# Two-layer encoder on one core: the last convolution block's taps as packed products on TensorE, and its input products moved between the first attention turns and the first scores

## The chip, the core and the metric

The program runs on one core of a Trainium2 chip. A core has five engines with a queue of instructions each, which it works off strictly in order: PE (TensorE, matrix products, whose results land in banks of an accumulator memory, PSUM, of 128 partitions by 512 float32), DVE (VectorE), ACT (ScalarE), POOL (GpSimd) and SP (SyncE, which here only starts DMA transfers). An instruction waits on semaphores for others; whatever is queued behind a waiting instruction on its engine waits too. The metric is the device time of one execution in microseconds (us).

## The reference, cut to what matters

Two layers on a sequence of 512 tokens with 1024 features. Each layer adds a gated feed-forward block (half weight), a "mix" of attention and convolution, and a second feed-forward block (half weight), and ends in a norm. The change is inside the mix:

```
h = rms_norm(x);  p = h @ w_in          # columns split: q latent, kv latent, k_pe, convolution
attn = mla_group(...)                    # 8 heads of 96, chunk-causal
u = a * sigmoid(g)                       # a, g: 512 channels each, from p
y[t, ch] = conv_b[ch] + sum_k conv_w[k, ch] * u[t - 30 + k, ch]     # 31 taps, causal, per channel
conv = silu(layer_norm(y))
x = x + concat(attn, conv) @ w_out
```

The convolution is depthwise: channel ch of y takes channel ch of u alone, at 31 shifts in time.

## The kernel before

Activations lie with features on the partitions and the 512 tokens along the free axis, so a shift in time is a shift along the free axis. The 512 convolution channels are four blocks of 128, named c0 to c3. A large product of float32 accuracy is made of three products with operands split into a high and a low part (`mm3`, L144, L145, L146); a projection of one block of 128 columns is 8 x 3 = 24 such products of 512 columns (`group`), and a weight tile takes a load on SP (L131), a cast on ACT (L133) and a subtraction on DVE or POOL (L139). For the first four tiles of w_out that subtraction is a second ACT pass (L136) and an accumulating DMA that POOL starts (L137).

The mix first runs its projections in the order of the string `SEQ`: q0 to q2, qo, k, kt, tt, uq, uk for attention (uk is `keys`, whose last step per token block is a power on POOL, `sck<-ssk`, L162, then the scaling of `kn` on DVE), and c0 to c3 for the convolution: `conv_in(c)` is two projections (48 products) and then `glu` (L510 DVE, L512 ACT, L514 and L516 DVE), which leaves u[c]. c0's products are the ones that come ahead of "R". Then come the heads, in a software pipeline over `step` (`ORDER` "t0s1p3v4o5"): in one step the code issues the turn of head step (L695, L700: transposes of q and kn on PE, evicted by ACT at L697 and DVE at L702), the scores of head step - 1 (L718, L719 on PE, row maximum L720 on DVE, exponential L724 on ACT), turn_p of head step - 3 (L739, L742), values of step - 4 (L752, L759) and turn_out of step - 5 (L770).

After the heads' code the convolution's taps are issued, as the string `CONV` = "DAAD" says for c0 to c3:

- Kind D: ACT writes weight times u plus bias into a PSUM bank of the tag "cv", which has one buffer (L787), DVE adds the 30 other taps into the bank one at a time (L791), and ACT copies it back (L801).
- Kind A: ACT writes the product of one tap into a buffer `pr` (L795; three buffers), and POOL adds it into y (L799). In c1 the adds from shift 16 on, and in c2 all of them, are told to issue only after the last `sck` of the keys.

Then POOL adds the four blocks (`ysum`, L813 to L815), a product with a matrix of ones takes the mean (`pm`, L817), and layer norm, silu and the products of w_out follow. `early` groups of w_out's attention half are put between these.

The order of each engine's queue is set when the program is built: a scheduler with a timeline of its own places the instructions by when it takes their operands to be ready. So code that stands after the heads, such as the taps, is spread between the heads' instructions. In the names below cv is a block's PSUM bank, r a general slot, pr and y as above, ps a PSUM bank, mx and sums the softmax's rows.

Of the kernel before, what the change touches and what calls it, by code (L numbers as in the profile page):

```python
# [7 lines left out]
FP = mybir.dt.float32  # L8
# [3 lines left out]
AF = mybir.ActivationFunctionType  # L12
# [3 lines left out]
P = 128  # L16
D = 1024
S = 512
L = 2
# [10 lines left out]
CK = 31  # L30
# [3 lines left out]
WC = 1024  # L34
# [3 lines left out]
FRB = 9  # L38
RING = 40
WIDE = 4  # L40
CONV = "DAAD"
PAUSE = 16
SEQ = "q0 R c1 q1 q2 qo k kt tt uq uk c2 c3"
POOLW = "wo"
QFOLD = 0
GLUP = 0
# [22 lines left out]

@with_exitstack  # L70
def encoder_kernel(ctx: ExitStack, tc: tile.TileContext, xT, consts, vecs, rgain, wgu1, wd1,
                   wcv, wql, wkl, wuq, wkv, wout, wgu2, wd2, out):
    nc = tc.nc
    PSUM = bass.MemoryType.PSUM
    cpool = ctx.enter_context(tc.tile_pool(name="const", bufs=1))
# [2 lines left out]
    wpool = ctx.enter_context(tc.tile_pool(name="w", bufs=4))  # L78
    rpool = ctx.enter_context(tc.tile_pool(name="rp", bufs=2))
    small = ctx.enter_context(tc.tile_pool(name="small", bufs=2))  # L80
    psum = ctx.enter_context(tc.tile_pool(name="psum", bufs=7, space=PSUM))
    uid = [0]

    def nm(s):
        uid[0] += 1
        return f"{s}{uid[0]}"

    def slot(dt=FP, w=S):
        return ring.tile([P, w], dt, tag="r", name=nm("r"))
# [4 lines left out]
    def bank():  # L94
        return psum.tile([P, S], FP, tag="ps", name=nm("ps"))
# [4 lines left out]
    V, A, G, T = nc.vector, nc.scalar, nc.gpsimd, nc.tensor  # L100
# [23 lines left out]
    def vv(l, name):  # L124
        o, w = VOFF[name]
        return vec[:, l, o:o + w]

    def load_w(src, w, kind="", two=False):
        raw = wpool.tile([P, WC], FP, tag="raw", name=nm("raw"), bufs=3)
        to = raw[:, :w]  # L130
        nc.sync.dma_start(out=to.rearrange("p (m c) -> p m c", m=2) if two else to, in_=src)  # L131
        hi = wpool.tile([P, WC], FR, tag="wh", name=nm("wh"))
        A.copy(hi[:, :w], raw[:, :w])  # L133
        lo = wpool.tile([P, WC], FR, tag="wl", name=nm("wl"))
        if kind == "sum":
            A.activation(lo[:, :w], raw[:, :w], AF.Copy, scale=-1.0)  # L136
            G.dma_start(out=lo[:, :w], in_=src, accum_op=ALU.add)  # L137
            return hi, lo
        (G if kind in POOLW.split() else V).tensor_tensor(lo[:, :w], raw[:, :w], hi[:, :w].bitcast(FP),  # L139
                                                          ALU.subtract)  # L140
        return hi, lo
# [6 lines left out]
    def split(src, w=S):  # L148
        hi, lo = slot(FR, w), slot(FR, w)
        A.copy(hi, src)  # L150
        V.tensor_tensor(lo, src, hi.bitcast(FP), ALU.subtract)
        return hi, lo
# [56 lines left out]
    def group(o, w, rhs, ks, n):  # L209

        for k in ks:
            c = slice(k * P, (k + 1) * P)
            mm3(o, w[0][:, c], w[1][:, c], rhs[k][0], rhs[k][1], k == 0, k == n - 1)
# [286 lines left out]
    def mix(l, gx, norm, done):  # L500
        with tc.tile_pool(name="k", bufs=4) as kpool:
            mix_body(kpool, l, gx, norm, done)

    def mix_body(kpool, l, gx, norm, done):
        u, order = [], {}
        ys = [None if kind == "D" else kpool.tile([P, S], FP, tag="y", name=nm("y"), bufs=2) for kind in CONV]

        def glu(pa, pg):
            tg = tmp()
            V.tensor_tensor(tg, pg, R, ALU.mult)  # L510
            sg = tmp()
            A.activation(sg, tg, AF.Sigmoid)  # L512
            ta = tmp()
            V.tensor_tensor(ta, pa, R, ALU.mult)  # L514
            uc = slot()
            (G if GLUP else V).tensor_tensor(uc, ta, sg, ALU.mult)  # L516
            u.append(uc)

        def conv_in(c):
            pp = []  # L520
            for j in range(2):
                ps = bank()
                group(ps, load_w(wcv[l, 2 * c + j], WC, f"c{c}"), gx, range(KD), KD)
                pp.append(ps)
            glu(*pp)
# [148 lines left out]
        rm = norm()  # L674
        for step in SEQ.split():
            if step == "R":
                R = norm()
# [85 lines left out]
        def turn_out(h):  # L763
# [6 lines left out]
                T.transpose(ps[:, t * P:(t + 1) * P], o[:, t * P:(t + 1) * P], ident)  # L770
            at.append(split(ps))

        STAGES = [({"t": turn, "s": scores, "p": turn_p, "v": values, "o": turn_out}[c], int(d)) for c, d in zip(ORDER[::2], ORDER[1::2])]
        for step in range(H + 6):
            for stage, lag in STAGES:
                if 0 <= step - lag < H:
                    stage(step - lag)


        with tc.issue_after(order["keys"]):  # L780
            wo = [load_w(wout[l, m], WC, "sum") for m in range(WOP)]
        cw, cb = vv(l, "cw"), vv(l, "cb")
        for c in range(4):
            kind = CONV[c]
            acc = psum.tile([P, S], FP, tag="cv", name=nm("cv"), bufs=1) if kind == "D" else ys[c]
            tap = lambda k: cw[:, c * CK + k:c * CK + k + 1]
            A.activation(acc, u[c], AF.Identity, scale=tap(CK - 1), bias=cb[:, c:c + 1])  # L787
            for k in range(CK - 2, -1, -1):
                s = CK - 1 - k
                if kind == "D":  # L790
                    V.scalar_tensor_tensor(acc[:, s:], u[c][:, :S - s], tap(k), acc[:, s:], ALU.mult, ALU.add)  # L791
                    continue
                pr = kpool.tile([P, S], FP, tag="pr", name=nm("pr"), bufs=3)
                if kind == "A":
                    A.activation(pr[:, s:], u[c][:, :S - s], AF.Copy, scale=tap(k))  # L795
                else:
                    G.tensor_scalar(pr[:, s:], u[c][:, :S - s], tap(k), None, ALU.mult)
                with tc.issue_after(order["keys"]) if s >= PAUSE or c > 1 else nullcontext():
                    order["conv"] = G.tensor_tensor(acc[:, s:], acc[:, s:], pr[:, s:], ALU.add).ins  # L799
            if kind == "D":  # L800
                A.copy(u[c], acc)  # L801
                ys[c] = u[c]
# [27 lines left out]
        cv = []  # L830
# [217 lines left out]
```

## Time and profile before

| what | value |
|---|---|
| runs, median (lowest to highest) | 1835.69 us (1835.47 to 1835.96), three runs |
| the profiled execution's own time | 1836.73 us |
| its span, first to last instruction | 1834.9 us |
| mean granted TensorE clock | 0.993 |
| busy: PE / DVE / ACT / POOL | 98% / 73% / 52% / 15% of the span |
| mix of layer 0: keys' last product issued | 431.73 us |
| mix of layer 0: turn of head 0 on PE | 453.72 us |
| mix of layer 0: first scores of head 3 on PE | 475.04 us |
| mix of layer 0: product `pm`, L817 | 518.22 us |

Times inside the run are counted from the span's start. A timeline row gives start, duration, engine, line, operation, tiles, and in square brackets the idle time of the engine just before it and what ended it. Records of one kind in a row are put together as "x4". PE's products overlap in the pipeline, so the distance from start to start, not the duration shown, is what one costs in a row of many. The two layers run the same code; the same stage of layer 1 lies about 909 us later. In the table of windows the columns after the stretch are its length, each engine's busy time (with its number of instructions), the granted clock as a share of full speed, the share of the DMA engines, and GB/s.

### The profile page before, as it was taken

The numbers are of one execution on the slowest core, as the hardware profiler recorded it, in microseconds if no ns is written. First come the engines' busy times: TensorE is split into PE (matmuls) and PEld (weight loads), VectorE is DVE, ScalarE is ACT, GpSimd is POOL, SyncE is SP. The second block draws the span as 40 slices with busy tenths as digits, with TensorE's granted clock in tenths as the row PEclk, the third lists the DMA queues.
The fourth block names the chain that finished last, engine by engine and source line by source line (L and its number), as shares of the span: only waits on it lengthen the run. The fifth ranks groups of instructions, "written<-read, shape, count | busy, mean of one in ns | idle before, by whom it ended". The sixth has DMA issues, their size and how long they took to land.

```text
span 1834.9 us, 22168 instructions
## 1 busy us (share of the span) xinstructions
PE 1793.2 (98%) x8512; PEld 1489.1 (81%) x8512; DVE 1347.8 (73%) x1803; ACT 948.6 (52%) x1471; POOL 279.0 (15%) x216
## 2 busy tenths in 40 slices
PE   8999999999999999999998999999999999999997
PEld 6888888888788888888877888888978788888885
DVE  8957876587957957866778667755988678577754
ACT  6534445467954634445644344444778455344442
POOL 4000000058931000000000000000688300000000
PEclk9999999999999999999999999999999999999998
DMA  8332322225134332322712332123250534323221
GB/s 294 107 123 89 117 70 69 92 87 136 25 127 106 108 123 93 105 99 69 229 66 92 107 103 92 69 71 112 76 149 1 164 89 126 115 81 115 69 70 58
DMA packets 58492, 187.95 MB, mean 102 GB/s; under 512 B 6033, under 2 KB 6417, under 8 KB 58385
## 3 DMA queue, kind: packets, MB, share of 16 engines
q1 hardware_dynamic: 54496, 173.56, 28.6%
q0 software_dynamic: 3456, 12.58, 3.9%
q8 instruction: 67, 1.10, 0.3%
q10 hardware_dynamic: 432, 0.38, 0.1%
q14 instruction: 41, 0.33, 0.1%
HBM read 184.40 MB, written 2.10 MB: 102 GB/s over the span
## 4 chain that ended last, share of the span: by engine, by line
PE 69%; issue 19%; DVE 7%; ACT 3%; POOL 2%; DMA 1%; SPq 0%; POOLq 0%; DVEq 0%; ACTq 0%
PE ps L144 21%; PE ps L146 21%; PE ps L145 20%; PE ps L752 2%; PE ps L365 1%; PE ps L718 1%; DVE wl L229 1%; ACT pr L795 1%; PE ps L739 1%; DVE fr L325 1%; DVE wl L139 1%; DVE cv L791 1%; POOL y L799 1%; POOL sck L162 0%; PE ps L182 0%
## 5 line engine op out<-in xcount | busy, mean ns | idle before, releaser
L144 PE MATMUL ps<-wh,r 128*128 128x512 f32 (+2 forms) x1392 | 525.2, 387 | 13.0 <-ACT wh L227 7.5
L145 PE MATMUL ps<-wl,r 128*128 128x512 f32 (+2 forms) x1392 | 534.5, 386 | 0.0
L146 PE MATMUL ps<-wh,r 128*128 128x512 f32 (+2 forms) x1392 | 532.1, 385 | 0.0
L227 ACT CAST wh<-fr 128x1024 fp32r<-128x1024 f32 x256 | 268.9, 1050 | 264.4 <-PE ps L146 141.3
L229 DVE TENSOR_TENSOR wl<-fr,wh 128x1024 fp32r<-128x1024 f32 x256 | 314.3, 1230 | 106.0 <-ACT wh L227 105.8
L146 PE MATMUL ps<-r,wl 128*128 128x512 f32 x1008 | 391.4, 389 | 0.5 <-POOL wl L139 0.5
L145 PE MATMUL ps<-r,wh 128*128 128x512 f32 x1008 | 391.4, 389 | 0.0
L144 PE MATMUL ps<-r,wh 128*128 128x512 f32 x1008 | 390.7, 393 | 0.3 <-ACT r L150 0.3
L144 PEld LDWEIGHTS ps<-wh,r 128*128 128x128 f32 x1392 | 262.4, 189 | 63.6 <-ACT wh L227 7.5
L145 PEld LDWEIGHTS ps<-wl,r 128*128 128x128 f32 x1392 | 262.5, 189 | 50.6 <-issue 0.5
L146 PEld LDWEIGHTS ps<-wh,r 128*128 128x128 f32 x1392 | 262.4, 188 | 50.2
L133 ACT CAST wh<-raw 128x1024 fp32r<-128x1024 f32 (+2 forms) x150 | 148.9, 997 | 217.8 <-issue 89.0
L146 PEld LDWEIGHTS ps<-r,wl 128*128 128x128 f32 x1008 | 189.2, 188 | 40.9 <-POOL wl L139 1.3
L145 PEld LDWEIGHTS ps<-r,wh 128*128 128x128 f32 x1008 | 189.2, 188 | 40.6 <-issue 1.4
L144 PEld LDWEIGHTS ps<-r,wh 128*128 128x128 f32 x1008 | 188.8, 188 | 40.9 <-ACT r L150 1.2
L139 DVE TENSOR_TENSOR wl<-raw,wh 128x1024 fp32r<-128x1024 f32 (+3 forms) x134 | 157.9, 1179 | 64.1 <-ACT wh L133 63.1
L162 POOL TENSOR_TENSOR rtok<-vtok,minus_half 128x4 f32<-128x4 f32 x9 | 11.1, 1230 | 1107.7 <-DVE vtok L188 1107.7
L443 DVE SCALAR_TENSOR_TENSOR x<-ps,x 128x512 f32<-128x512 f32 x128 | 88.2, 689 | 111.4 <-PE ps L146 110.7
L799 POOL TENSOR_TENSOR y<-y,pr 128x509 f32<-128x509 f32 (+15 forms) x120 | 157.7, 1316 | 50.2 <-ACT pr L795 42.9
L325 DVE TENSOR_TENSOR fr<-fr,fr 128x1024 f32<-128x1024 f32 x112 | 135.3, 1219 | 7.7 <-DMA fr<-in_wgu 7.2
L355 ACT ACTIVATE e<-e,rtok 128x256 f32<-128x256 f32 x120 | 61.0, 509 | 111.5 <-DVE e L346 111.2
L341 ACT COPY e<-ps 128x512 f32<-128x512 f32 x120 | 70.3, 587 | 64.1 <-PE ps L146 63.9
(165 smaller groups left out, 1731.9 us busy)
## 6 DMA issues: line engine op xcount, KB each, us to landing
fr<-in_wgu SPq DMA_DIRECT2D x176, 512.0 KB, 4.0
raw<-in_wd SPq DMA_DIRECT2D x64, 512.0 KB, 4.2
raw<-in_wd SPq DMA_DIRECT2D x32, 384.0 KB, 3.2
raw<-in_wcv SPq DMA_DIRECT2D x16, 512.0 KB, 3.3
raw<-in_wout SPq DMA_DIRECT2D x16, 512.0 KB, 3.7
raw<-in_wgu SPq DMA_DIRECT2D x8, 512.0 KB, 4.2
fr<-in_wgu POOLq DMA_DIRECT2D x8, 512.0 KB, 7.0
raw<-in_wgu POOLq DMA_DIRECT2D x8, 512.0 KB, 7.6
```

Of the source, the lines that this page charges most:

```text
L133: A.copy(hi[:, :w], raw[:, :w])
L139: (G if kind in POOLW.split() else V).tensor_tensor(lo[:, :w], raw[:, :w], hi[:, :w].bitcast(FP), ALU.subtract)
L144: T.matmul(o, lh, rh, start=first, stop=False, skip_group_check=free)
L145: T.matmul(o, lh, rl, start=False, stop=False, skip_group_check=free)
L146: T.matmul(o, ll, rh, start=False, stop=last, skip_group_check=free)
L227: A.copy(hi[:, :w], src[:, :w])
L229: V.tensor_tensor(lo[:, :w], src[:, :w], hi[:, :w].bitcast(FP), ALU.subtract)
L325: V.tensor_tensor(oh, ah, bh, ALU.add)
L341: A.copy(w[:, j, :N], o[j][:, :N])
L355: A.activation(out[j][:, :h], src[j][:, :h], AF.Silu, scale=r)
L443: V.scalar_tensor_tensor(x[:, m, :], pd, 0.5, x[:, m, :], ALU.mult, ALU.add)
L799: order["conv"] = G.tensor_tensor(acc[:, s:], acc[:, s:], pr[:, s:], ALU.add).ins
```

## The change

`CONV` becomes "DAAP", and a new function makes the taps of c3 (kind P) on TensorE. A block of 128 channels is cut into four groups of 32. For group g a tile z of 128 partitions is filled with four copies of these 32 channels of u[3], shifted by 0, 1, 2 and 3 tokens (a memset of the first four columns on DVE, four DMA transfers of 64 KB from SP). A stationary operand of 128 x 32 holds four taps of each of the 32 channels on a diagonal, so one float32 product does four taps of 32 channels; with the moving operand z cut to its first 512 - 4i columns and the output shifted by 4i, eight products (i = 0 to 7) do all 31 taps, the 32nd being zero. The four groups write to partitions 0, 32, 64 and 96 of the same "cv" bank: 32 products, in an order in which the group changes from each to the next. The weights are laid out on the host (`wtap`), one tile of 512 KB a layer, in a buffer of the weights' tag "raw" and unsplit. ACT evicts the bank with the bias into a slot (L790), and the rest of the convolution uses it as y of c3.

The products of c2's input move ahead, to between q2 and qo; those of c3's input move from after the keys to after the turn of head 1, ahead of the scores of head 0; `packed(3)` is issued at the end of step 2, behind the scores of head 1.

```diff
-CONV = "DAAD"
+CONV = "DAAP"
-SEQ = "q0 R c1 q1 q2 qo k kt tt uq uk c2 c3"
+SEQ = "q0 R c1 q1 q2 c2 qo k kt tt uq uk"
...
-        ys = [None if kind == "D" else kpool.tile([P, S], FP, tag="y", name=nm("y"), bufs=2) for kind in CONV]
+        ys = [None if kind in "DP" else kpool.tile([P, S], FP, tag="y", name=nm("y"), bufs=2) for kind in CONV]
...
+        def packed(c):
+
+            w = wpool.tile([P, WC], FP, tag="raw", name=nm("raw"), bufs=3)
+            nc.sync.dma_start(out=w, in_=wtap[l])
+            acc = psum.tile([P, S], FP, tag="cv", name=nm("cv"), bufs=1)
+            zs = []
+            for g in range(4):
+                t = slot()
+                V.memset(t[:, 0:4], 0.0)
+                for j in range(4):
+                    nc.sync.dma_start(out=t[32 * j:32 * j + 32, j:S], in_=u[c][32 * g:32 * g + 32, 0:S - j])
+                zs.append(t)
+            for i in range(8):
+                for g in range(4):
+                    T.matmul(acc[32 * g:32 * g + 32, 4 * i:S], w[:, (g * 8 + i) * 32:(g * 8 + i + 1) * 32],
+                             zs[g][:, 0:S - 4 * i], start=i == 0, stop=i == 7, skip_group_check=True)
+            y = slot()
+            A.activation(y, acc, AF.Identity, bias=cb[:, c:c + 1])
+            ys[c] = y
+
+        cw, cb = vv(l, "cw"), vv(l, "cb")
         STAGES = [...]
         for step in range(H + 6):
             for stage, lag in STAGES:
                 if 0 <= step - lag < H:
                     stage(step - lag)
+                if stage is turn and step == 1:
+                    conv_in(3)
+            if step == 2:
+                packed(3)
...
-        cw, cb = vv(l, "cw"), vv(l, "cb")
         for c in range(4):
             kind = CONV[c]
+            if kind == "P":
+                continue
...
+    taps = np.zeros((L, 4, 32, 4, 8, 32), f32)
+    last = a["conv_w"][:, ::-1, 3 * P:].reshape(L, CK, 4, 32)
+    for k in range(CK):
+        for c in range(32):
+            taps[:, k % 4, c, :, k // 4, c] = last[:, k, :, c]
+    taps = taps.reshape(L, P, WC)
...
+        "wtap": taps, "wql": cols(w_in[:, :, :o1]), "wkl": rows(w_in[:, :, o1:o3]),
```

In the changed file the taps' lines move: the memsets are L781, the copies L783, the packed products L787, their eviction L790; kind D's start is L813, its taps L817, the copy back L827; kind A's products are L821 and POOL's adds L825; `ysum` is L839 to L841 and `pm` L843. Lines up to L770 keep their numbers.

PE in layer 0, where the keys' products end and the heads begin. Before, the last rows of c3's input (bank ps_3663) stand ahead of the turns of heads 0 and 1 (L695 on q, L700 on kn, four transposes each) and the first score:

```order
L146 MATMUL ps_3663<-r_2798,wl_3668 128x512
L695 MATMUL ps_3704<-cst,q_2814 96x128 x4
L700 MATMUL ps_3711<-cst,kn_2815 96x128 x4
L695 MATMUL ps_3718<-cst,q_2814 96x128 x4
L700 MATMUL ps_3725<-cst,kn_2815 96x128 x4
L718 MATMUL ps_3732<-r_3716,r_3709 128x128
```

The same place after: the last of the keys' products (bank ps_3612), the turns of heads 0 and 1 as far as kn of the first token block, and then the products of c3's input (bank ps_3662):

```order
L146 MATMUL ps_3612<-wh_3520,r_3324 128x512
L695 MATMUL ps_3634<-cst,q_2814 96x128 x4
L700 MATMUL ps_3641<-cst,kn_2815 96x128
L695 MATMUL ps_3648<-cst,q_2814 96x128 x4
L700 MATMUL ps_3655<-cst,kn_2815 96x128
L144 MATMUL ps_3662<-r_2564,wh_3665 128x512
```

The remaining transposes of kn stand between the second 24 of these 48 products, one token block after another; the 48 products of c2 now stand before the keys'.

ACT in layer 0 between the scores of heads 0 and 3, before. Exponentials (L724) and an eviction of a turn (L697) alternate with tap products (L795):

```order
L795 ACTIVATE pr_4445<-r_3630,vec 128x511
L724 ACTIVATE r_3739,sums_3735<-ps_3734,mx_3736 128x512
L697 ACTIVATE r_3761<-ps_3756,gqs_3702 96x512
L795 ACTIVATE pr_4448<-r_3630,vec 128x510
L724 ACTIVATE r_3774,sums_3735<-ps_3770,mx_3773 128x128
L795 ACTIVATE pr_4451<-r_3630,vec 128x509
L724 ACTIVATE r_3775,sums_3735<-ps_3771,mx_3773 128x384
```

ACT after, at the eviction of the packed products; it is the end of a run of fifteen tap products in a row (c1's 484 to 482, then c2's 511 to 500):

```order
L821 ACTIVATE pr_4533<-r_3149,vec 128x502
L821 ACTIVATE pr_4536<-r_3149,vec 128x501
L821 ACTIVATE pr_4539<-r_3149,vec 128x500
L790 ACTIVATE r_3852<-cv_3795,vec 128x512
L697 ACTIVATE r_3859<-ps_3854,gqs_3632 96x512
L724 ACTIVATE r_3873,sums_3871<-ps_3868,mx_3872 128x128
L724 ACTIVATE r_3874,sums_3871<-ps_3869,mx_3872 128x384
L724 ACTIVATE r_3875,sums_3871<-ps_3870,mx_3872 128x512
L742 COPY r_3900<-ps_3899 128x512
L821 ACTIVATE pr_4542<-r_3149,vec 128x499
L813 ACTIVATE cv_4381<-r_2947,vec 128x512
```

The eviction of head 3's qT (r_3859) and the exponentials of head 2 (mx_3872) now stand behind these fifteen and behind the eviction of the packed bank; c0's start (L813) follows it, since it needs the same bank.

PE after, behind the packed products: the end of them, turn_p of head 0, head 4's turn, the last score of head 2 (bank ps_3868, whose first part the exponential above has to free) and the first score of head 3 (from r_3859):

```order
L787 MATMUL cv_3795<-r_3814,raw_3793 32x484
L739 MATMUL ps_3906<-cst,r_3738 128x128
L739 MATMUL ps_3906<-cst,r_3739 128x128
L695 MATMUL ps_3911<-cst,q_2814 96x128 x4
L700 MATMUL ps_3918<-cst,kn_2815 96x128 x4
L718 MATMUL ps_3868<-r_3768,r_3761 128x256
L719 LDWEIGHTS mrow
L719 MATMUL ps_3868<-mneg,mrow 128x64
L718 MATMUL ps_3925<-r_3866,r_3859 128x128
```

What the two scores read comes out of ACT's queue behind L790.

DVE: c0's taps. Before, they start right behind u[0] (r_2947), in the stretch of the projections:

```order
L516 TENSOR_TENSOR r_2947<-t_2945,t_2943 128x512
L791 SCALAR_TENSOR_TENSOR cv_4320<-r_2947,vec,cv_4320 128x511
L791 SCALAR_TENSOR_TENSOR cv_4320<-r_2947,vec,cv_4320 128x510
L139 TENSOR_TENSOR wl_3109<-raw_3105,wh_3107 128x864
L791 SCALAR_TENSOR_TENSOR cv_4320<-r_2947,vec,cv_4320 128x509
```

After, they start among the row maxima of head 3 and fill the heads' second half, where c3's taps were:

```order
L720 TENSOR_REDUCE mx_3872<-ps_3868 128x1
L720 TENSOR_REDUCE mx_3928<-ps_3925 128x1
L720 TENSOR_REDUCE mx_3928<-ps_3926 128x1
L817 SCALAR_TENSOR_TENSOR cv_4381<-r_2947,vec,cv_4381 128x511
L720 TENSOR_REDUCE mx_3928<-ps_3927 128x1
L817 SCALAR_TENSOR_TENSOR cv_4381<-r_2947,vec,cv_4381 128x510
```

All thirty of c0's taps thus moved behind the eviction L790. Layer 1's queues show the same shapes at these places.

More of the change, by code (lines that the diff above doesn't have):

```diff
@@ L71, in encoder_kernel @@
 def encoder_kernel(ctx: ExitStack, tc: tile.TileContext, xT, consts, vecs, rgain, wgu1, wd1,
-                   wcv, wql, wkl, wuq, wkv, wout, wgu2, wd2, out):
+                   wcv, wtap, wql, wkl, wuq, wkv, wout, wgu2, wd2, out):
     nc = tc.nc
@@ L1033 @@
         "wcv": cols(np.concatenate([ca, cg], 3).reshape(L, D, 2 * CW)),
-        "wql": cols(w_in[:, :, :o1]), "wkl": rows(w_in[:, :, o1:o3]),
+        "wtap": taps, "wql": cols(w_in[:, :, :o1]), "wkl": rows(w_in[:, :, o1:o3]),
         "wuq": rows(a["w_uq"]), "wkv": rows(kv), "wout": cols(a["w_out"]),
```

## The prediction

> **What bounds the kernel now.** I read the page's totals first, then the two mixes by windows, then the timeline of PE, and last the timelines and groups of the engines that PE waits for there.
>
> ```profile
> span 1834.9 us, 22168 instructions
> PE 1793.2 (98%) x8512; PEld 1489.1 (81%) x8512; DVE 1347.8 (73%) x1803; ACT 948.6 (52%) x1471; POOL 279.0 (15%) x216
> ```
>
> PE is the bound over the whole run; 42 us of idle are left. The change touches only the mixes, so the average decides nothing. The windows of the heads' first part (turn of head 0 to first scores of head 3) and of the rest (to `pm`), for layer 0 and layer 1:
>
> ```profile
> core 0: us, PE busy (x) PEld busy (x) DVE busy (x) ACT busy (x) POOL busy (x), PEclk, DMA share, GB/s
> 453.72:475.04 21.32, 15.83 (x87) 10.51 (x86) 17.21 (x32) 21.29 (x47) 20.18 (x18) 0.92 0.45 100
> 475.04:518.22 43.18, 42.40 (x332) 36.84 (x331) 35.49 (x69) 33.33 (x83) 33.23 (x27) 1.00 0.00 1
> 1362.67:1383.82 21.15, 16.79 (x87) 11.69 (x86) 18.90 (x33) 20.95 (x46) 20.01 (x17) 0.84 0.41 94
> 1383.82:1427.19 43.37, 42.58 (x330) 37.03 (x331) 34.70 (x68) 33.09 (x81) 32.55 (x27) 1.00 0.01 2
> ```
>
> In the first part ACT is busy 21.29 of 21.32 us and POOL 20.18: these two set its pace and PE idles 5.5 and 4.4 us. The rest is PE-bound, with DVE at 35.5 of 43.2. PE around both, and layer 1's first score of head 3 and `pm`:
>
> ```profile
> 431.96 0.39 PE L144 MATMUL ps<-r,wh 128*128 128x512 f32 x1
> ...
> 453.49 0.39 PE L146 MATMUL ps<-r,wl 128*128 128x512 f32 x1
> 453.72 0.60 PE L695 MATMUL ps<-cst,q 128*96 128x128 f32 x4
> ...
> 459.74 0.49 PE L718 MATMUL ps<-r,r 96*128 96x128 f32 x2 [4.11 <-ACT r L697]
> ...
> 475.04 0.39 PE L718 MATMUL ps<-r,r 96*128 96x128 f32 x2
> ...
> 1383.82 0.46 PE L718 MATMUL ps<-r,r 96*128 96x128 f32 x2 [0.50 <-DVE r L742]
> ```
>
> From 431.96 to 453.72 stand the 96 products of c2 and c3: 0.227 us each, 10.9 us for 48. POOL beside them: the keys' `sck`, the first DMA start behind them in each layer, and an add near the first part's end:
>
> ```profile
> 434.23 5.25 POOL L162 TENSOR_TENSOR sck<-ssk,minus_half 128x8 f32<-128x8 f32 x3
> 440.47 2.76 POOL L162 TENSOR_TENSOR sck<-ssk,minus_half 128x8 f32<-128x8 f32 x1 [0.99 <-DVE scp L666]
> 443.18 0.92 POOL L137 DMA_DIRECT2D wl<-in_wout  x1
> 443.84 3.31 POOL L799 TENSOR_TENSOR y<-y,pr 128x496 f32<-128x496 f32 x2
> ...
> 478.04 2.59 POOL L799 TENSOR_TENSOR y<-y,pr 128x503 f32<-128x503 f32 x2 [0.38 <-ACT pr L795]
> ```
> ```profile
> 1350.87 0.91 POOL L137 DMA_DIRECT2D wl<-in_wout  x1
> ```
>
> POOL gets to its adds 11.3 us after the keys' products (443.18 - 431.96) and takes about 1.25 us an add from then on; the 24 adds down to c2's 503 take from 443.2 to 479.3, 36.1 us with four DMA starts between. Because `pr` has three buffers, ACT can't run ahead of POOL by more than three products.
>
> **The change, part by part.** The sum is made against the profiled execution, 1836.73 us, which lies 1.04 us above the runs' median.
>
> 1. *c2's products ahead of the keys'.* PE's work is the same. All that follows the keys' products comes 10.9 us later: they end at 442.8 instead of 431.9. c3's 48 products fill the wait for `kn` that now stands behind the keys. So PE gains the first part's idle and pays elsewhere; what it pays is read at the first score of head 3, which takes both in.
>
> 2. *POOL.* The adds from shift 16 on issue only behind the last `sck`. These came with lags set by PE, DVE and POOL together. Upper bound: the same lag, 454.1. Lower: with c2's `glu` already done on DVE, four `sck` of 1.75 us (5.25 / 3) from the first token block's sum at about 441.7, 448.7. I take 448.7, since nothing but the keys' own chain is left on DVE and ACT there; so 5.5 us later than before, and in layer 1 the same, 1350.9 + 5.5 and by its own keys' end 5.9.
>
> 3. *ACT's queue.* Head 3's qT, head 2's exponentials and L790 stand behind c2's products down to 500, which needs the add of 503, the 24th behind the last `sck`.
>
> ```profile
> L799 POOL TENSOR_TENSOR y<-y,pr x120: 1205/1254/2103, 389.1 to 1413.7; 128x511 f32<-128x511 f32 x4, 128x510 f32<-128x510 f32 x4, 128x509 f32<-128x509 f32 x4, 128x508 f32<-128x508 f32 x4
> ```
> ```profile
> L724 ACT ACTIVATE r<-ps,mx 128x512 f32<-128x512 f32 x16 | 11.2, 698 | 0.4 <-DVE mx L720 0.4
> L697 ACT ACTIVATE r<-ps,gqs 96x512 f32<-96x512 f32 x16 | 10.9, 690 | 0.2 <-PE ps L695 0.2
> ...
> L724 ACT ACTIVATE r<-ps,mx 128x128 f32<-128x128 f32 x16 | 5.9, 371 | 0.1
> L787 ACT ACTIVATE cv<-r,vec 128x512 f32<-128x512 f32 x4 | 3.1, 779 | 1.7 <-DVE r L516 1.7
> L795 ACT ACTIVATE pr<-r,vec 128x500 f32<-128x500 f32 x4 | 3.0, 746 | 0.0
> ```
>
> 24 x 1.25 + 4 x 0.66 (443.84 - 443.18) = 32.6 us at the least, 36.1 as before at the most; I take 35, near the second, since ACT serves the same adds. 448.7 + 35 = 483.7. Then, from start to start about 0.1 under the durations: the product 500 (0.6), L790 (0.7, priced as the bank's start L787), L697 (0.6), the first exponential (0.3), and head 2's last score (0.5): head 3's first score at 486.4. Before it was 475.04: **+11.4 us in layer 0**. In layer 1, whose POOL starts at 1350.87: 1350.87 + 5.9 + 35 + 2.7 = 1394.5, plus 0.9 for a first part that was slower by its clock: 1395.4 against 1383.82, **+11.6**. PE stands idle in that time for want of work, since `turn_p`, values and the scores of all later heads hang on those exponentials or stand behind them in its queue.
>
> 4. *The packed product.* Its copies on SP wait for the memsets, which stand on DVE behind head 1's last row maximum, about 464.
>
> ```profile
> L960 SPq DMA_DIRECT2D out_T<-r x8: 332/332/348, 1826.8 to 1831.4; - x8
> ```
> ```profile
> out_T<-r SPq DMA_DIRECT2D x8, 256.0 KB, 2.2
> ...
> raw<-in_wout SPq DMA_DIRECT2D x16, 512.0 KB, 3.7
> ```
>
> 16 starts of 0.33 us are 5.3, the last lands 2.2 later (256 KB from this memory; 3.7 for a weight's 512 KB): the operands are there at about 471.8. The weights' 512 KB and the copies' 1 MB a layer cost nothing, since SP and the DMA queues have the heads' second part almost empty (share 0.00 above); SP's wout loads stand partly behind the copies, and are wanted only past 518. The product itself has no row. The nearest is a float32 product of the full array, `pm`:
>
> ```profile
> 517.73 0.66 PE ps L770 x4
> 518.39 0.86 PE ps L817 x2
> ```
>
> One product of 512 columns, two records, 0.86 us. The 32 have 498 columns in the mean (512 - 4i over eight): 32 x 0.86 x 498/512 = 26.8 us if they run one behind the other, 6.7 if four go side by side in the array's strips of 32 columns. I take 10, nearer to the second, since consecutive ones name different strips and share no output. Until L790's turn comes on ACT at 484.3 up to 12.5 us are free (484.3 - 471.8): the cover is the idle time of part 3, and the term is **0**. Without that cover it would be 10 a layer. The Trainium skill, page "TensorE: Matmul & The Clock Gate", Part 3 on packing small matmuls, states 2.38 times the speed for three tiles of 32 output columns by 512; by it the product takes 26.8 / 2.38 = 11.3 us, an estimate, and the sum stays; by the row above alone it would be 60 us more over both layers (rival B). No row here shows products side by side.
>
> 5. *DVE.* c3's thirty taps go, but c0's start (L813) needs the one "cv" bank, so all thirty come behind L790 and none lies under the projections any more.
>
> ```profile
> core 0: us, DVE busy (x), PEclk, DMA share, GB/s
> 453.72:475.04 21.32, 7.16 (x10) 0.92 0.45 100
> 475.04:518.22 43.18, 14.64 (x21) 1.00 0.00 1
> ```
>
> The second part had 21 taps at 0.69 us, now 30: 35.5 + 9 x 0.69 = 41.7 of 43.2 us. With so little room some evictions come late: bounds 0 and 9 taps whole, 6.2; I take **+2 a layer**, near the lower, as the taps fill gaps. The memsets (four of 4 columns) are under 1 us beside PE's idle.
>
> 6. *ysum.* c0 now ends last: copy back, then three adds, and `pm` stands in PE's queue ahead of the early groups.
>
> ```profile
> L801 ACT COPY r<-cv x4: 582/638/682, 413.4 to 1411.4; 128x512 f32<-128x512 f32 x4
> ```
> ```profile
> 506.79 1.27 POOL L813 TENSOR_TENSOR t<-r,y 128x512 f32<-128x512 f32 x1
> 508.13 1.27 POOL L814 TENSOR_TENSOR t<-t,y 128x512 f32<-128x512 f32 x1
> 509.49 1.27 POOL L815 TENSOR_TENSOR t<-t,r 128x512 f32<-128x512 f32 x1
> ```
>
> Before, ysum was done at 510.8, 7.4 us ahead of `pm`. Now the last tap stands just ahead of the last L759 on DVE: 0.64 + 3 x 1.3 = 4.5 us, of which 1.4 lies beside L759 and L770: **+3.1 a layer** (0 if the taps end 3 us earlier, 4.5 if later).
>
> 7. *Clock.* PE's idle lowers the granted clock:
>
> ```profile
> 455.40:459.74 4.34, 0.23 (x4) 0.00 (x1) 1.77 (x3) 4.34 (x8) 4.18 (x5) 1.00 0.99 203
> 460.00:465.00 5.00, 5.00 (x21) 3.02 (x21) 4.40 (x9) 4.97 (x11) 4.69 (x5) 0.66 0.76 138
> 1370.00:1375.00 5.00, 5.00 (x18) 3.19 (x16) 4.89 (x9) 4.99 (x12) 4.78 (x4) 0.50 0.28 59
> ```
>
> After 4.3 us idle, 5 us ran at 0.66 of the clock, in layer 1 at 0.50. That price, 1.7 to 2.5 us, goes from the first part and comes back behind the new wait, where PE is the bound: **+1 a layer** (0 to 2.5). Against it stands head 4's turn, which PE does during the wait: **-0.9 a layer** (eight transposes of 0.11).
>
> Sum: 11.4 + 11.6 + 2 x (2 + 3.1 + 1 - 0.9) = 33.4; 1836.73 + 33.4 = 1870.1, and by the median 1869.
>
> **The rivals.**
>
> *B, the packed products run one behind the other.* For it: every fp32 product in the trace that follows another costs its full time. Against: none of these names a part of the columns. It decides once the product passes 12.5 us. At 26.8 it ends at 498.6, head 3's first score is at 500.8, +25.8 a layer, with the other terms as above (less of the taps' price, the DVE having waited too): 1836.7 + 2 x (25.8 + 4) = 1896.
>
> *C, faster: ACT isn't held.* The first part's idle and its slow clock are filled by c3's products (5.5 + 4.4 us of idle and 1.7 + 2.5 of clock, 14.1 over both layers), and the packed product lies in what the exponentials leave. Place: ACT's queue ahead of L790. It decides if ACT's products come through before PE runs out of work, some 14 us earlier than in part 3: POOL's last `sck` near 435, or adds at 0.85 us. Then two products of 3.3 us not hidden: 1836.7 - 14.1 + 6.7 = 1829. Against it: the adds never took less than 1.205 us, and the keys' products come later, not earlier.
>
> *D, the hold is half as long*, since the scheduler's operands come earlier and POOL reaches its adds at once: +5 a layer in part 3 and +3 behind it: 1853. The 32.6 us of part 3 speaks for some of it, but gives 2.4 a layer only.
>
> **How the numbers follow.** My forecast (ACT held at POOL's pace, product hidden): chance 0.62, 1869, its own range 1856 to 1882 from parts 3 and 5 to 7 at their ends. B 0.22, 1889 to 1903. D 0.08. C 0.08, of which 0.05 gains over 0.2% and 0.03 lies within it (0.2% is 3.7 us, about what a measurement of this kernel can tell from no change). Range 1850 to 1898: it takes in D and most of B and leaves out C. Faster 0.05, same 0.03, slower 0.92.
>
> **What would show it.** Right: on PE a wait of over 10 us ahead of head 3's first score, put down to ACT (r L697 or r L724); ACT in that stretch nothing but `pr` products waiting for POOL; L790 without a wait on PE; c0's taps behind it to the end of the heads; a short wait at `pm` for ysum. Wrong: L787 as a block of over 13 us with ACT waiting at L790 for PE (B), or a first score of head 3 earlier than 478 (C).

## The result, and the profile after

The changed kernel takes 1877.25 us in the median (1876.19 to 1878.56, four runs) against 1835.83 us before: 1.0226 of it, 95% interval 1.0208 to 1.0243, so 41.4 us slower. The forecast was 1869, range 1850 to 1898. The profiled execution took 1878.56 us. Its page begins:

```profile
span 1876.4 us, 22441 instructions
PE 1822.6 (97%) x8640; PEld 1497.8 (80%) x8640; DVE 1310.0 (70%) x1751; ACT 955.2 (51%) x1469; POOL 272.9 (15%) x216
```

The span grew by 41.5 us, PE's busy time by 29.4. DVE lost 38 us of work, and the time went up all the same. PE around the packed products (L787), head 3's first score and `pm` in layer 0, on the timeline of after:

```profile
470.75 1.05 PE L787 MATMUL cv<-r,raw 128*32 128x512 f32 x2
473.00 1.02 PE L787 MATMUL cv<-r,raw 128*32 128x512 f32 x2 [1.20 <-DMA r<-r]
475.43 1.89 PE L787 MATMUL cv<-r,raw 128*32 128x512 f32 x2 [1.42 <-DMA r<-r]
478.06 8.79 PE L787 MATMUL cv<-r,raw 128*32 128x512 f32 x58 [0.75 <-DMA r<-r]
486.79 0.44 PE L739 MATMUL ps<-cst,r 128*128 128x128 f32 x2
488.21 0.64 PE L695 MATMUL ps<-cst,q 128*96 128x128 f32 x4 [0.98 <-ACT r L697]
...
489.59 0.46 PE L718 MATMUL ps<-r,r 96*128 96x128 f32 x2
...
537.26 2.07 PE L843 MATMUL ps<-t,onesm 128*128 128x512 f32 x2 [3.05 <-POOL t L841]
```

From 470.75 to 486.79 PE does nothing but the packed products, and it starts them one tile of copies at a time. The wait that I had forecast ahead of head 3's first score, over 10 us for ACT, isn't there: PE waits 0.98 us for ACT, since until then it is held by the packed products and their operands (DMA in the brackets), which come earlier in its queue. ACT in the same stretch:

```profile
485.61 0.71 ACT L821 ACTIVATE pr<-r,vec 128x500 f32<-128x500 f32 x1 [0.62 <-POOL y L825]
486.90 0.69 ACT L790 ACTIVATE r<-cv,vec 128x512 f32<-128x512 f32 x1 [0.57 <-PE cv L787]
487.48 0.67 ACT L697 ACTIVATE r<-ps,gqs 96x512 f32<-96x512 f32 x1
```

ACT does run its taps at POOL's pace, and ends them at 486.3; the packed products end 0.5 us later. In layer 1 the order is the other way round. There the packed products end at 1412.4, ACT's taps 2.2 us later, L790 follows them without a wait for PE, and PE waits 3.03 us for ACT:

```profile
1405.56 6.84 PE L787 MATMUL cv<-r,raw 128*32 128x512 f32 x58 [1.59 <-DMA r<-r]
...
1415.80 0.64 PE L695 MATMUL ps<-cst,q 128*96 128x128 f32 x4 [3.03 <-ACT r L697]
```
```profile
1413.88 0.71 ACT L821 ACTIVATE pr<-r,vec 128x500 f32<-128x500 f32 x1 [0.61 <-POOL y L825]
1414.50 0.67 ACT L790 ACTIVATE r<-cv,vec 128x512 f32<-128x512 f32 x1
```

The two chains end within 0.5 us of each other in layer 0 and 2.2 us in layer 1, so the trace by itself can't say which one is the cause.

The windows from head 3's first score to `pm` (layer 0, layer 1), then the clock behind that score in layer 1 and behind `pm` in layers 0 and 1:

```profile
core 0: us, PE busy (x) PEld busy (x) DVE busy (x) ACT busy (x) POOL busy (x), PEclk, DMA share, GB/s
489.59:537.26 47.67, 43.19 (x332) 36.92 (x330) 42.63 (x80) 33.39 (x82) 25.87 (x21) 0.99 0.01 2
1417.18:1467.06 49.88, 46.04 (x333) 39.11 (x331) 42.80 (x80) 33.79 (x82) 26.49 (x22) 0.91 0.00 1
1417.18:1423.20 6.02, 6.02 (x21) 3.95 (x20) 4.12 (x8) 6.02 (x16) 4.56 (x5) 0.51 0.00 1
537.26:545.00 7.74, 7.74 (x19) 5.47 (x20) 4.47 (x7) 2.61 (x5) 0.00 (x0) 0.60 0.00 0
1467.06:1475.00 7.94, 7.94 (x23) 5.73 (x24) 4.47 (x7) 2.61 (x5) 0.00 (x0) 0.70 0.00 0
```

To divide the 41.5 us between the layers, a mark in layer 0's second feed-forward block (L365), first the row of before, then that of after:

```profile
L365 PE MATMUL ps<-cst,e x20: 270/272/273, 593.7 to 634.2; 128*128 128x128 f32 x20
```
```profile
L365 PE MATMUL ps<-cst,e x8: 270/272/272, 615.8 to 618.8; 128*128 128x128 f32 x8
```

Layer 0 loses 22.1 us: 14.55 up to head 3's first score (489.59 against 475.04), 4.49 from there to `pm` (47.67 against 43.18), and the other 3.1 behind it. Layer 1 loses 19.4: 11.3 up to that score (1417.18 against 1383.82, less the 22.1 brought along), 6.5 to `pm` (49.88 against 43.37), 1.6 behind.

### The profile page after: what moved, and what is told of

Same layout as the page of the kernel before. It is cut to its first block, busy times and chain, and to the rows that moved or that the text cites. A ratio compares the mean times of both kernels' runs of the same rounds, so it can differ in the third digit from the quotient of the medians.

```text
span 1876.4 us, 22441 instructions
## 1 busy us (share of the span) xinstructions
PE 1822.6 (97%) x8640; PEld 1497.8 (80%) x8640; DVE 1310.0 (70%) x1751; ACT 955.2 (51%) x1469; POOL 272.9 (15%) x216
## 4 chain that ended last, share of the span: by engine, by line
PE 74%; issue 18%; DVE 4%; ACT 2%; POOL 2%; DMA 0%; SPq 0%; POOLq 0%; DVEq 0%; ACTq 0%
PE ps L144 22%; PE ps L146 22%; PE ps L145 22%; PE ps L752 2%; PE ps L718 2%; PE ps L365 1%; DVE wl L229 1%; PE ps L739 1%; POOL y L825 1%; PE cv L787 0%; PE ps L182 0%; DVE fr L325 0%; ACT pr L821 0%; ACT r L724 0%; PE ps L700 0%
## 5 line engine op out<-in xcount | busy, mean ns | idle before, releaser
L139 DVE TENSOR_TENSOR wl<-raw,wh 128x1024 fp32r<-128x1024 f32 (+3 forms) x134 | 160.3, 1199 | 94.8 <-ACT wh L133 93.8
L825 POOL TENSOR_TENSOR y<-y,pr 128x509 f32<-128x509 f32 (+15 forms) x120 | 158.0, 1319 | 56.2 <-ACT pr L821 49.4
```

## The experiments

Each run is timed beside the kernel before on its own chip (1835.3 to 1835.8 us).

**The packed products left out.** In `packed`:

```diff
-            zs = []
...
+            for g in range(4):
+                T.matmul(acc[32 * g:32 * g + 32, :], w[:, g * 256:g * 256 + 32],
+                         u[c], start=True, stop=True, skip_group_check=True)
```

> The changed kernel with the sixteen shifted copies, the four memsets and 28 of the 32 packed products left out: four products on u[3] itself write the bank, so three taps in four of the last block are not computed. In its ACT queue the eviction of the bank and head 2's exponentials now stand behind c1's tap 485, fifteen tap products earlier than in the changed kernel. Theory 1 (the prediction's: ACT is held by POOL's adds, and the packed product costs nothing of its own): little changes, 1870 to 1878 us. Theory 2 (the place of the packed product's eviction in ACT's queue makes the hold; POOL's pace alone holds nothing back): head 3's first score goes from 489.6 to about 477, about 11 us a layer, 1853 to 1860 us. What stays above before, then, is c0's lateness.

Measured: 1840.80 us (1.0024, 1.0015 to 1.0034), 36.5 us under the changed kernel and below both ranges. Theory 1's forecast is missed by 30 us: the packed products and what hangs on them are nearly all of the loss. But the run of fifteen taps no longer stands ahead of the eviction either (ACT evicts the bank at 467.11, behind tap 485), so this run takes both chains away and doesn't tell them apart. Theory 2 pointed the right way but was too small, since head 3's first score comes even earlier than before (row below against 475.04). What is left stands at `pm`:

```profile
470.38 0.39 PE L718 MATMUL ps<-r,r 96*128 96x128 f32 x2
...
518.48 2.07 PE L835 MATMUL ps<-t,onesm 128*128 128x512 f32 x2 [3.00 <-POOL t L833]
```

**c0's taps first.** The loop over the taps becomes a function, called for c0 ahead of the heads:

```diff
+        conv_taps(0)
         STAGES = [...]
...
-        for c in range(4):
-            kind = CONV[c]
+        for c in range(1, 4):
+            conv_taps(c)
```

> The changed kernel with c0's thirty taps issued ahead of the heads, so that they take the cv bank first and lie under the projections, as before the change. ACT's run of taps ahead of the packed eviction stays. Prediction's terms 5 to 7: the wait ahead of pm goes (3.05 us in layer 0, 3.06 in layer 1), the half clock behind it too (about 3 us a layer), and DVE has room in the heads' second part: 5 to 8 us a layer, 1861 to 1867 us; head 3's first score stays near 489. Rival (taps on DVE in the second part cost nothing, ysum waits for POOL or ACT instead): 1874 to 1878 us.

Measured: 1865.36 us (1.0161, 1.0146 to 1.0176), 11.9 us less than the changed kernel, 5.9 a layer, as expected. Head 3's first score stays (490.41), `pm` follows the last transposes at once, and behind it the clock is whole where it was 0.60:

```profile
490.41 0.46 PE L718 MATMUL ps<-r,r 96*128 96x128 f32 x2
...
533.59 0.66 PE L770 MATMUL ps<-cst,t 128*128 128x128 f32 x4 [0.78 <-DVE t L759]
534.09 1.02 PE L847 MATMUL ps<-t,onesm 128*128 128x512 f32 x2
```
```profile
534.09:542.00 7.91, 7.91 (x39) 6.30 (x38) 5.23 (x9) 4.33 (x7) 0.34 (x1) 1.00 0.00 0
```

**The moved inputs alone.**

```diff
-CONV = "DAAP"
+CONV = "DAAD"
...
-            if step == 2:
-                packed(3)
```

> Only the second half of the change: c2's input ahead of the keys, c3's input between the turn of head 1 and the scores of head 0; all taps as before (DAAD), nothing packed. Theory 1 (POOL's adds, which start 5.5 us later against the heads, hold ACT): head 3's first score at 486 or later, about 1858 us. Theory 2 (POOL's pace holds nothing where exponentials and tap products alternate in ACT's queue, and c3's products fill the first part's idle of 5.5 and 4.4 us and its slow clock): 1822 to 1834 us, faster than before.

Measured: 1842.55 us (1.0036, 1.0023 to 1.0049): between the two ranges. Up to head 3's first score the move gains 2.8 us (472.20), so POOL's later start holds nothing there in this kernel; the loss stands at `pm`, where this time POOL itself is late, its adds running without a gap:

```profile
479.68 35.48 POOL L823 TENSOR_TENSOR y<-y,pr 128x508 f32<-128x508 f32 x27 [0.38 <-ACT pr L819]
515.12 1.27 POOL L837 TENSOR_TENSOR t<-r,y 128x512 f32<-128x512 f32 x1
...
517.80 1.26 POOL L839 TENSOR_TENSOR t<-t,r 128x512 f32<-128x512 f32 x1
```
```profile
472.20 0.39 PE L718 MATMUL ps<-r,r 96*128 96x128 f32 x2
...
519.12 2.08 PE L841 MATMUL ps<-t,onesm 128*128 128x512 f32 x2 [2.98 <-POOL t L839]
```

**The packed taps alone.**

```diff
-SEQ = "q0 R c1 q1 q2 c2 qo k kt tt uq uk"
+SEQ = "q0 R c1 q1 q2 qo k kt tt uq uk c2 c3"
...
-                if stage is turn and step == 1:
-                    conv_in(3)
```

> Only the first half of the change: the packed taps, with both inputs ahead of the heads as before. In ACT's queue sixteen tap products in a row stand ahead of the packed eviction, c0's taps come last on DVE. PE's work of 9 us a layer for the packed products, the idle for the run of taps, and c0's lateness are all here, and nothing fills the first part's idle. Theory 2: head 3's first score comes 12 to 16 us later than before, and 5 to 7 us more behind it: 1870 to 1882 us, as the whole change. Theory 1 (the moved inputs make POOL late): with POOL's adds where they were before, 3 to 6 us a layer less than the whole change, 1864 to 1871 us.

Measured: 1885.10 us (1.0270, 1.0255 to 1.0285), 49.3 us over before, 7.9 over the whole change, and above both ranges. Theory 1's forecast is missed again: with POOL's last `sck` done at 442.1, as early as before the change, it is slower, not faster. But ACT's hold is not gone. Fifteen taps in a row stand ahead of L790 here too, only nine taps further on, and in layer 0 they end last, 1.0 us behind the packed products (488.94):

```profile
489.35 0.70 ACT L819 ACTIVATE pr<-r,vec 128x491 f32<-128x491 f32 x1 [0.61 <-POOL y L823]
489.96 0.67 ACT L790 ACTIVATE r<-cv,vec 128x512 f32<-128x512 f32 x1
```

The packed taps cost 49 us without the move; the move takes 8 of them back.

**ACT freed of POOL's pace.** c2's tap products are told to issue on ACT behind L790:

```diff
-            A.activation(y, acc, AF.Identity, bias=cb[:, c:c + 1])
+            order["packed"] = A.activation(y, acc, AF.Identity, bias=cb[:, c:c + 1]).ins
...
-                    A.activation(pr[:, s:], u[c][:, :S - s], AF.Copy, scale=tap(k))
+                    with tc.issue_after(order["packed"]) if c == 2 else nullcontext():
+                        A.activation(pr[:, s:], u[c][:, :S - s], AF.Copy, scale=tap(k))
```

> The changed kernel with c2's tap products on ACT told to issue behind the packed eviction (L790), so that nothing of POOL's pace stands between c1's last tap and L790; copies, packed products and everything else as in the changed kernel. Theory A (the prediction's: the run of taps at POOL's pace holds ACT, so L790 and what is behind it come earlier without it): L790 at about 479, head 3's first score near 481, 1858 to 1866 us. Theory B (the packed product, late by its sixteen copies, ends at the same time as the run and holds L790 by itself): head 3's first score stays at 488 to 491; c2's adds start 17 us later on POOL, so a wait at pm of the same size or more: 1876 to 1886 us.

Measured: 1876.66 us (1.0223, 1.0206 to 1.0240), the changed kernel's time. ACT now stands idle for 15.75 us ahead of L790, waiting for PE, and head 3's first score is where it was, at 488.46:

```profile
485.76 0.69 ACT L790 ACTIVATE r<-cv,vec 128x512 f32<-128x512 f32 x1 [15.75 <-PE cv L787]
```

So the run of taps at POOL's pace, which the prediction took for the cause, isn't needed for the loss: it fills a wait that is there without it. In layer 1 it is the same: ACT waits 14.91 us ahead of L790, which starts at 1414.16 in place of 1414.50.

**The same with four copies in place of sixteen.**

```diff
-            for g in range(4):
+            for g in range(1):
                 t = slot()
                 V.memset(t[:, 0:4], 0.0)
...
-                             zs[g][:, 0:S - 4 * i], ...
+                             zs[0][:, 0:S - 4 * i], ...
```

> As the run with c2's taps behind the packed eviction, and only four of the sixteen copies: one tile of shifted channels serves all four groups, so the last block's channels 32 to 127 take the first 32's input; the 32 products are all done. Twelve starts of 0.67 us and their landing go. Theory B: the first packed product waits once, all 32 end at about 479, head 3's first score at 480 to 482, 8 us a layer less than the run with sixteen copies. Theory C (neither the run nor the copies: the product's own time on PE holds it, nine us a layer and more): no more than 2 us a layer less.

Measured: 1856.88 us (1.0116, 1.0101 to 1.0131), 19.8 us less than with sixteen (1876.66), 9.9 a layer, as theory B has it, which forecast 8. Three of the four memsets go with the twelve copies. SP's starts on the timeline, first of after, then of this run, and this run's PE and ACT:

```profile
465.65 10.78 SPq L783 DMA_DIRECT2D r<-r  x16
```
```profile
464.55 2.50 SPq L783 DMA_DIRECT2D r<-r  x4
```
```profile
469.51 6.89 PE L787 MATMUL cv<-r,raw 128*32 128x512 f32 x64 [0.81 <-DMA r<-r]
...
479.15 0.47 PE L718 MATMUL ps<-r,r 96*128 96x128 f32 x2
```
```profile
476.45 0.69 ACT L790 ACTIVATE r<-cv,vec 128x512 f32<-128x512 f32 x1 [6.70 <-PE cv L787]
```

A start of such a copy takes 10.78 / 16 = 0.67 us. Thirty-two packed products take 6.9 us; that is 3.9 times as fast as the 26.8 us of the prediction's serial price.

**A buffer of its own for the evicted block.**

```diff
-            y = slot()
+            y = kpool.tile([P, S], FP, tag="yp", name=nm("yp"), bufs=1)
```

> The changed kernel with the packed eviction's output in a buffer of its own in place of a slot of the ring that the heads' operands use. In every kernel with the slot, head 3's qT eviction (the next one to take a slot) stands right behind L790 in ACT's queue; in this one it and head 2's and 3's exponentials stand ahead, alternating with taps, and PE's packed products are spread between scores. Theory D (the slot's place in the ring made the hold): head 3's first score at 471 to 476, PE pays the packed products' 7 to 9 us behind it, and c0's taps still end last: 1858 to 1868 us. Theory A or B (POOL's pace or the copies hold ACT or PE anyway): 1874 to 1880 us.

Measured: 1871.45 us (1.0195, 1.0179 to 1.0210), 5.8 us less: short of theory D's range and below its rivals'. What D says of the first scores is there: head 3's comes at 472.64, and PE does the last 29 packed products behind it, from 482.34. But c0's taps now start later against the heads, and `pm` gives most of it back:

```profile
472.64 0.39 PE L718 MATMUL ps<-r,r 96*128 96x128 f32 x2
...
482.34 6.87 PE L787 MATMUL cv<-r,raw 128*32 128x512 f32 x58
...
535.38 2.08 PE L843 MATMUL ps<-t,onesm 128*128 128x512 f32 x2 [9.72 <-POOL t L841]
```

The slot would explain ACT's order. In all kernels here whose evicted block takes a slot, the next instruction of ACT is head 3's L697, the next to take one; with its own buffer, L697 and the exponentials go ahead. That a ring of slots is given out in program order, and so ties the heads' operands to L790, is the reading that fits all of them; only the edit and its effect are measured.

**Both: own buffer, and c0's taps first.**

> The changed kernel with both mended: the packed eviction's own buffer, and c0's taps ahead of the heads. Left of the change are the moved inputs, and on PE the packed products. From the order-only run (1842.6, of which some 6 us a layer are its wait at pm and the slow clock behind it): 1842.6 - 12 + 2 x 8.5 for the packed products = 1848, 1844 to 1854 us. If c0's lateness and the hold overlapped: 1855 to 1862.

Measured: 1851.34 us (1.0086, 1.0071 to 1.0101), as expected, 25.9 us under the changed kernel. Alone the two edits gave 5.8 and 11.9; together 8 more, because each hides part of the other's wait. Against before head 3's first score is 1.6 us earlier (473.48) and `pm` 7.7 later (525.90 against 518.22), with no wait ahead of either. What is left is PE's own work: between the two it is busy for 51.64 us, 9.2 more than the 42.40 before, and 31 of the 32 packed products, some 8.7 us of PE, lie there.

```profile
473.48 0.39 PE L718 MATMUL ps<-r,r 96*128 96x128 f32 x2
...
525.90 1.02 PE L847 MATMUL ps<-t,onesm 128*128 128x512 f32 x2
```
```profile
473.48:525.90 52.42, 51.64 (x395) 39.13 (x394) 24.08 (x48) 37.95 (x88) 42.13 (x34) 1.00 0.08 20
```

**The moved inputs with POOL relieved.** On the order-only kernel:

```diff
-PAUSE = 16
+PAUSE = 24
-YP = 1
+YP = 0
...
-        G.tensor_tensor(ysum, ys[0], ys[1], ALU.add)
-        G.tensor_tensor(ysum, ysum, ys[2], ALU.add)
+        V.tensor_tensor(ysum, ys[0], ys[1], ALU.add)
+        V.tensor_tensor(ysum, ysum, ys[2], ALU.add)
```

> The order-only kernel (nothing packed, taps DAAD, c2's input ahead of the keys, c3's between the turn of head 1 and the scores of head 0), and POOL relieved: adds of c1 up to shift 23 in place of 15 may issue ahead of the last sck, and the three ysum adds go to DVE. In the order-only run POOL's adds ran without a gap from 479.7 to 515.2, and pm waited 2.98 us for them. Theory E (POOL's late adds are all that the order-only run loses behind head 3's first score): eight adds of 1.25 us fewer end POOL at about 505, no wait at pm, 2 x (3.7 + 2.7) us less than 1842.6: 1828 to 1832 us, faster than before. Rival (c3's taps on DVE, or the early c2, cost the heads' second part): 1836 to 1842 us.

Measured: 1859.15 us (1.0126, 1.0110 to 1.0141), 16.6 us slower than without, both expectations missed. Head 0's first score comes 7.0 us later than in the order-only run (464.39 against 457.41), so most of the loss, 8.3 us a layer, stands ahead of the heads. The early adds stand in POOL's queue around the sums of a norm of the mix (L177), which PE waits for ahead of L182, 2.53 us against 0.64:

```profile
390.13 27.06 POOL L823 TENSOR_TENSOR y<-y,pr 128x511 f32<-128x511 f32 x18 [21.51 <-ACT pr L819]
417.15 1.98 POOL L177 TENSOR_TENSOR acc<-acc,t 128x512 f32<-128x512 f32 x1
```
```profile
422.31 1.87 PE L182 MATMUL ps<-ones,acc 128*128 128x1 f32 x8 [2.53 <-POOL acc L177]
```

That is a part of the 7.0 us; the rest isn't traced here. `pm` still waits, 2.09 us, now for the sum on DVE.

**Only c3's input moved.** On the order-only kernel, c2 back behind the keys:

```diff
-SEQ = "q0 R c1 q1 q2 c2 qo k kt tt uq uk"
+SEQ = "q0 R c1 q1 q2 qo k kt tt uq uk c2"
```

> Only c3's input is moved (between the turn of head 1 and the scores of head 0); c2's stays behind the keys, as before the change; nothing packed. kn is ready when PE gets to the turns, so c3's products lie between turns and scores with nothing to wait for, and POOL's adds keep their distance from the keys. Theory E: the first part's idle of 4 us and its slow clock are filled, no wait at pm beyond 1 us: 1824 to 1832 us. Rival (c3's later input makes its taps on DVE end last, and pm waits for them): 1834 to 1842 us.

Measured: 1829.67 us (0.9970, 0.9959 to 0.9982): 5.6 us faster than before, and faster than every other kernel here. Head 3's first score comes 1.1 us earlier than before and `pm`, without a wait, 1.05:

```profile
473.93 0.39 PE L718 MATMUL ps<-r,r 96*128 96x128 f32 x2
...
517.17 1.02 PE L841 MATMUL ps<-t,onesm 128*128 128x512 f32 x2
...
1421.54 1.02 PE L841 MATMUL ps<-t,onesm 128*128 128x512 f32 x2
```

In layer 1 `pm` is at 1421.54 against 1427.19, 5.65 earlier, 1.05 of it brought along.

**Both: c3's input alone moved, POOL relieved.**

> Both: only c3's input moved, and POOL relieved as in the run with early adds. If POOL or ysum was what held pm in either: 1822 to 1830 us, the fastest. If the eight early adds push the sck behind them on POOL and make kn late: 1830 to 1838 us.

Measured: 1850.84 us (1.0083, 1.0069 to 1.0096): the two edits cost 21 us here, more than was expected. The reason shown for the run above isn't it: PE doesn't wait for L177's sums at 406.80. The last `sck` is done at 449.1 against 442.9 without the edits, as the second expectation feared; PE also waits 3.43 us for a weight's subtraction on DVE (L139) and 2.09 us at `pm` for the sum on DVE. Neither run tells the early adds' share from that of the sum on DVE.

## Why the prediction was right, and where not

The direction and the range held, by the case that was given 0.62, and 33.4 us were forecast of 41.4. But the step that named the cause failed, and the price of that step, 11.4 and 11.6 us for the two layers against 14.55 and 11.3 measured, came out near by luck: a second chain, which the prediction took to be hidden, ends at almost the same time.

- *Step 3, ACT's queue held at POOL's pace: there as a chain, failed as the cause.* The queue and the pace are as read: fifteen taps in a row, 35 us forecast from the last `sck` to the last of them (448.7 to 483.7), 37.9 in the trace (448.4 to 486.3). In layer 1 this chain even ends last. But the loss doesn't hang on it: with c2's taps behind L790 nothing changes (1876.66). In its place: PE, whose queue puts the packed products ahead of head 4's turn, waits for sixteen copies and is held until 486.8; L790 needs the last packed product; and L697 and the exponentials stand behind L790, by the reading above because the evicted block takes a slot of the heads' ring. That the scheduler lays the run of taps into the time that the packed products take is a reading that fits three runs (no run of taps ahead of the eviction without them, nine taps further on with POOL's adds early, a wait in its place with the taps behind L790), no more. No run takes the copies away and leaves the run of taps in its place; by the trace it would by itself have held L790 until 486.3.
- *Step 4, the packed product at 0: failed, and the term mis-sized is the copies.* Its own time was near: 10 us taken, 6.9 measured at the full clock, so it doesn't run one behind the other, as rival B had it. The copies were priced too low: 0.33 us a start by an output's row, 0.67 measured, and as the groups take turns, each of the first three tiles let in one product only. The last tile came at 478.1, not 471.8, so of the 12.5 us of cover nothing was left in layer 0. Copies cost 9.9 us a layer, measured between 16 and 4 with the taps out of the way. The product's own time shows in the kernel with both edits, 16.0 us over before. The Trainium skill, page "TensorE: Matmul & The Clock Gate", Part 3 on packing small matmuls, gives 2.38 times for three column tiles; the four here, in float32, ran 3.9 times as fast as the serial estimate.
- *The sign for rival B* came for another reason than B's. L787 fills 16 us in layer 0, over the 13 named, and ACT waits at L790 for PE (0.57 us), but 7.3 us of the 16 go by before the last tile of copies is there.
- *Step 1, c3's products fill the wait for kn: right.* The prediction gave this gain no price of its own. The move alone brings head 3's first score in layer 0 2.8 us ahead of before. Rival C counted 14.1 us for it over both layers; the move alone ended 6.7 us above before, lost at `pm`.
- *Step 2, the last `sck`: right* (448.7 forecast, 448.4 measured), but in the order-only run the later POOL costs nothing at head 3's first score, only at `pm`.
- *Steps 5 to 7, c0 last, ysum and the clock: right in kind, too small.* 5.2 us a layer forecast, 7.6 and 8.1 measured behind head 3's first score. The wait at `pm` was 3.05 us for 3.1 forecast. The term that was mis-sized is the clock: 1 us a layer taken, but behind each of three waits of 3 us PE ran 6 to 8 us at 0.51 to 0.70, 2.4 to 3.1 us lost each time. Nor did the 0.9 us come that were taken off for head 4's turn: PE does it at 488.21, behind the hold. c0's taps first took back 11.9 us in all.

## What to carry to other kernels

Where two chains end together, the trace names one of them; take each away by itself before calling it the cause, look whether the order of the queues changed with the edit, and expect two edits to give more together than apart. A tile that is handed from a shared ring may tie instructions that share no data, so try a buffer of its own for an output that comes late. When work moves to an engine that is the bound, look for the part of the change that fills that engine's gaps and keep it alone: here moving one projection gained 5.6 us, and the packing lost all of it many times over.

## What the runs showed of the hardware

- Float32 products with 32 output rows, aimed in turn at four column strips, ran nearly side by side: 32 of them, 498 columns in the mean, in 6.89 us at the full clock, where one full product of 512 columns takes 0.86 us.
- A copy of 64 KB within the on-chip memory took 0.67 us to start on SP's queue, twice an output's 0.33, and landed in 1.9 us, little sooner than the output's 256 KB (2.1 in the same trace):

```profile
r<-r SPq DMA_DIRECT2D x8, 64.0 KB, 1.9
```

- A wait of 0.98 us on PE ahead of head 4's turn in layer 0 left the clock whole (1.00 from 490 to 497), one of 3.03 us at the same place in layer 1 halved it for 6 us (0.51). But the length of one wait isn't all: the last 29 packed products, behind three waits of 0.75 to 1.42 us with one product between, ran at 0.77 in layer 0 and took 8.79 us; in layer 1, behind three of 1.41 to 1.59 us, they ran at 1.00 and took 6.84.
